# Reordered sums, copies and casts around seven-product units, and the last row statistic in three pieces, in a two-layer decoder trunk on one core

## The chip, the cores and the metric

The kernel runs on one core of one Trainium2 chip. Its time is the device time of one execution in microseconds; a comparison uses the median of several. The engines are named as in the profile: PE (TensorE), DVE (VectorE), ACT (ScalarE), POOL (GpSimd) and SP (SyncE, which issues most DMAs). Each engine works through its own queue in order, and waits where an operand is not ready.

## The reference, cut to what matters

```python
for i in range(2):
    h = h + 0.5 * swiglu(rmsnorm(h, norm_ffn1[i]), ffn1_w_in[i], ffn1_w_out[i])
    h = h + (retention if i == 0 else gla)(rmsnorm(h, norm_mix[i]), ...)
    h = h + 0.5 * swiglu(rmsnorm(h, norm_ffn2[i]), ffn2_w_in[i], ffn2_w_out[i])
return rmsnorm(h, final_norm)[:, 16:]

def swiglu(x, w_in, w_out):
    gate, up = split(x @ w_in, 2)
    return (silu(gate) * up) @ w_out
```

h has 528 rows (16 learned tokens and 512 of the input) of 1024 float32 values; the hidden width of swiglu is 2816, 22 tiles of 128. So there are four feed-forward blocks, called f10, f20, f11 and f21 in order of time, with retention after f10 and gated linear attention after f11.

## The kernel before, in words

Everything is kept transposed: features on the 128 partitions, tokens along the free dimension, in two halves of 264 (in f21 of 256). A float32 product is made of three products in a reduced format: a matrix is cast to a high part (ACT, L187: whi) and the rest is subtracted (DVE, L188: wlo); PE multiplies high by high (L487), high by low (L488) and low by high (L489).

Most products are taken in pairs of weight tiles by a scheme that needs seven block products instead of eight. Such a group is a *unit*. Its products have the names a11, s1, s2, a12, s4, s3, a22: sums of blocks of the weights (the tile `pair` holds two such sums, added up by a POOL DMA, L154; L194 and L196 make two more out of raw tiles) times sums of blocks of the activations. In a feed-forward block there are gate units ("g"), u units ("u", the up half) and o units ("o", the output). A product of a g or u unit is four tiles of three PE products, 12 in all.

The results of the seven lie in three pieces of PSUM: a bank X and two halves of QZ. X is used four times in a unit: a11, s2, s3 and a22 in turn. So X has to be read before the next of these can begin: a11 and s2 are copied to scratch by ACT (L734, L729), s1 by L727; s3 and a22 are read straight into a sum. The scratch tile is called su or szf. Three callbacks take the sums: `row1` after s4 (reads scratch and QZ), `c22` after s3 (reads X and scratch), `c21` after a22 (reads X). In a u unit `row1` adds (L1022) and multiplies by the gate's row (L1023), `c22` adds (L1030) and multiplies (L1031), `c21` is L1034. In an o unit `c22` adds scratch (L1068) and then X (L1069) to the residual x, and `c21` is L1073. The seventh product, a22, of a held unit stands on PE behind the next unit's a11 and s1. In the order of most units s4 comes before s3; in the last u unit of a block s3 comes first.

After each product `step` calls `hook()`, which fetches weights some products ahead (their casts and splits, L187 and L188), and then takes the results. Results are issued at high priority. In a block's very first unit the copies are issued ahead of the fetch, and the casts are told to stand behind the copy (`W.after`). A scheduler lays the instructions out in each engine's queue by these priorities and by when it takes their operands to be ready.

At the end (`out_last`) the rest of the last o products is taken in two halves of the tokens. For the second half each of the eight tiles x[d] is squared by ACT (L1190), and DVE adds the squares up (L1193) except the last; PE transposes the gained tiles (L1242) into yt, and column sums of the summed squares and of the last square, two PE instructions each, give the row statistic st_fb (L1249). After it come its root on POOL (L461), the scaling (ACT L1266 for rows 0 to 127, DVE L1268 for the others) and the writes (L1269).

Of the kernel before, what the change touches and what calls it, by code (L numbers as in the profile page):

```python
# [268 lines left out]
def trunk(ctx, tc, a):  # L269
# [422 lines left out]
    def unit_steps(key, name, order, halves, ks, rhs, places, row1, c22, c21, behind=None, done=None):  # L692
# [49 lines left out]
        def step(q, part=None):  # L742
# [72 lines left out]
    def ffn(which, layer, halves, gcol, u, feed, late=False):  # L815
# [7 lines left out]
        with tc.tile_pool(name=f"h_{me}", bufs=1) as hp, tc.tile_pool(name=f"t_{me}", bufs=1) as tp, \  # L823
# [187 lines left out]
            def unit_u(f, g, first):  # L1011
                y = []
# [6 lines left out]
                def row1(ab, qz):  # L1019
                    begin()  # L1020
                    o = y[0][:, 2:]
                    V.tensor_add(o, ab, qz)  # L1022
                    V.tensor_mul(o, o, pair(g[0], halves))  # L1023
# [3 lines left out]
                def c22(c, s):  # L1027
                    begin()
                    o = y[0][:, 1]
                    V.tensor_add(o, c, s)  # L1030
                    V.scalar_tensor_tensor(o, o, -1.0, g[1][:, b0:b1], ALU.mult, ALU.mult)  # L1031

# [14 lines left out]
            def unit_o(gi, d, behind):  # L1047
# [18 lines left out]
                def c22(c, s):  # L1066
                    o = x[d + 1][:, b0:b1]
                    V.scalar_tensor_tensor(o, s, 0.5, o, ALU.mult, ALU.add)  # L1068
                    V.scalar_tensor_tensor(o, c, 0.5, o, ALU.mult, ALU.add)  # L1069
# [102 lines left out]
    def out_last(key, hh, hl, halves, scale):  # L1172
# [10 lines left out]
        def evac(d, hf):  # L1183
# [4 lines left out]
            else:  # L1188
                t = tmp.tile([P, T], F32, tag="hf", name=f"sqf{hf}_{d}")
                S.activation(t[:, :wd], x[d][:, r0:r1], AF.Square)  # L1190
                if (d, hf) == (KD - 1, 1):
# [34 lines left out]
        later(1, lambda: later(1, rsqrt_rows(sqa[0][:, :wd], 1, D, "fa", first_half)[0]))  # L1226
        for d in range(KD - tail, KD):
# [5 lines left out]
            last = evac(d, 1)  # L1233
# [5 lines left out]

        def turn(d):  # L1240
            for j in range(2):
                nc.tensor.transpose(yt[j][:, d // 4, (d % 4) * P:(d % 4 + 1) * P], xg[d][:, j * P:(j + 1) * P], ident)  # L1242

        for d in range(KD - 4):
            turn(d)
        st = bank("st_fb")
        for i, sq in enumerate((sqa[1], last)):
            for j in range(2):
                ins = nc.tensor.matmul(st[:, j:j + 1], lhsT=sq[:, j * P:(j + 1) * P], rhs=ones[:, 0:1],  # L1249
                                       start=(i + j == 0), stop=(i == 1), skip_group_check=True)  # L1250
        with tc.issue_after(ins.ins):
            for d in range(KD - 4, KD):
# [5 lines left out]
        for b in range(2):  # L1258
            for j in range(2):
# [3 lines left out]
                for o in (0, 256) if b + j == 0 else (0,):  # L1263
                    c = slice(o, 256 + o if b + j == 0 else 512)
# [4 lines left out]
                    (nc.scalar if b + j == 2 else nc.sync).dma_start(  # L1269
# [1067 lines left out]
```

## Time and profile before

| | |
|---|---|
| three runs, us | 2020.34, 2024.03, 2027.34 (median 2024.03) |
| the profiled execution's own time, us | 2026.07 |
| its span, first to last instruction, us | 2024.3 |
| mean granted TensorE clock | 0.998 |
| DMA, mean over the span | 158 GB/s |

A row of the timeline has the start, the length, the engine, the line, the operation, what it writes and reads, and in brackets how long its engine idled before it and what ended that. A row of waits has the engine and tile that waited, what it waited for, the total in us, how many times, and the longest. PE is pipelined: a product is still shown when the next has started.

### The profile page before, as it was taken

How to read it: one execution, taken by the hardware profiler on the slowest of the kernel's cores; microseconds unless marked ns; L12 is line 12 of the kernel's file. 1: busy time of each engine (PE TensorE's matmuls, PEld its weight loads, DVE VectorE, ACT ScalarE, POOL GpSimd, SP SyncE). 2: the span in 40 equal slices, each digit the busy share in tenths (PEclk: the TensorE clock that was granted, in tenths of full speed). 3: DMA queues.
4: the chain of work that ended last, by engine and by line, in shares of the span. 5: the costliest groups of instructions: out<-in, count | busy, mean ns of one | idle time of the engine just before them, and what ended most of it. 6: DMA issues, size and time to landing. Idle time of an engine off the chain costs nothing.

```text
span 2024.3 us, 43498 instructions
## 1 busy us (share of the span) xinstructions
PE 1998.4 (99%) x16575; PEld 1965.3 (97%) x16575; DVE 1792.3 (89%) x3302; ACT 1192.3 (59%) x2427; POOL 209.9 (10%) x181
## 2 busy tenths in 40 slices
PE   9999999999999999999999999999999999999998
PEld 8999999999999999999999999999999989999998
DVE  8999999978787889989999998999997878988996
ACT  5666666554545465656666666667644544655664
POOL 1011111010101000111111011111001000111110
PEclk9999999999999999999999999999999999999999
DMA  7577777354645532776875477777624441687772
GB/s 227 136 198 178 200 192 185 109 146 132 159 129 147 136 115 74 191 191 161 214 188 162 128 190 187 179 199 178 187 65 119 112 135 63 165 202 183 181 189 68
DMA packets 176113, 318.87 MB, mean 158 GB/s; under 512 B 17568, under 2 KB 40736, under 8 KB 175904
## 3 DMA queue, kind: packets, MB, share of 16 engines
q1 hardware_dynamic: 133856, 237.04, 36.1%
q0 software_dynamic: 40896, 75.51, 23.4%
q10 hardware_dynamic: 1152, 3.55, 0.6%
q8 instruction: 130, 2.13, 0.4%
q14 instruction: 79, 0.65, 0.1%
HBM read 311.76 MB, written 4.26 MB: 156 GB/s over the span
## 4 chain that ended last, share of the span: by engine, by line
PE 80%; DVE 13%; ACT 2%; issue 2%; DMA 2%; POOL 0%; SPq 0%; POOLq 0%; DVEq 0%; ACTq 0%
DVE wlo L188 4%; PE po_r L488 1%; PE po_r L487 1%; PE po_r L489 1%; ACT whi L187 1%; PE lv L1857 1%; PE Xf11u L487 1%; PE Xf11u L489 1%; PE Xf11u L488 1%; PE Xf11g L487 1%; PE Xf11g L488 1%; PE Xf11g L489 1%; PE Xf20u L487 1%; DVE raw L196 1%; DVE hf L520 1%
## 5 line engine op out<-in xcount | busy, mean ns | idle before, releaser
L187 ACT CAST whi<-raw 128x512 fp32r<-128x512 f32 (+1 forms) x893 | 531.1, 606 | 415.0 <-DVE raw L196 151.4
L188 DVE TENSOR_TENSOR wlo<-raw,whi 128x512 fp32r<-128x512 f32 (+1 forms) x893 | 589.8, 668 | 101.2 <-ACT whi L187 88.6
L187 ACT CAST whi<-pair 128x512 fp32r<-128x512 f32 (+1 forms) x304 | 183.6, 604 | 77.4 <-issue 10.9
L188 DVE TENSOR_TENSOR wlo<-pair,whi 128x512 fp32r<-128x512 f32 (+1 forms) x304 | 201.7, 664 | 15.9 <-ACT whi L187 14.8
L154 POOL DMA_DIRECT2D pair<-in_f_in x73 | 89.0, 1220 | 714.7 <-DVE wlo L188 286.0
L194 DVE TENSOR_TENSOR raw<-pair,raw 128x512 f32<-128x512 f32 (+1 forms) x146 | 97.1, 665 | 5.7 <-DMA pair<-in_f_in 2.5
L196 DVE TENSOR_TENSOR raw<-raw,raw 128x512 f32<-128x512 f32 (+1 forms) x146 | 97.3, 666 | 3.2
L154 POOL DMA_DIRECT2D pair<-in_f_out x44 | 53.5, 1216 | 357.1 <-DVE wlo L188 101.0
L488 PE MATMUL po_r<-ogl,whi 128*128 128x264 f32 x256 | 71.3, 278 | 0.0
L487 PE MATMUL po_r<-ogh,whi 128*128 128x264 f32 x256 | 71.2, 278 | 0.0
L489 PE MATMUL po_r<-ogh,wlo 128*128 128x264 f32 x256 | 71.2, 278 | 0.0
L154 POOL DMA_DIRECT2D pair<-in_ret_in x20 | 24.4, 1222 | 300.6 <-DVE wlo L188 138.3
L997 ACT ACTIVATE gf<-gf 128x528 f32<-128x528 f32 (+1 forms) x36 | 23.2, 643 | 50.6 <-DVE gf L996 50.4
L487 PE MATMUL Xf10o<-hf,whi 128*128 128x264 f32 x176 | 49.6, 282 | 1.0 <-ACT szf L734 0.4
L487 PE MATMUL Xf20o<-hf,whi 128*128 128x264 f32 x176 | 49.4, 281 | 1.1 <-ACT szf L734 0.4
L487 PE MATMUL Xf11o<-hf,whi 128*128 128x264 f32 x176 | 49.4, 280 | 1.1 <-ACT szf L734 0.4
L488 PE MATMUL Xf10o<-hf,whi 128*128 128x264 f32 x176 | 49.1, 279 | 0.0
L488 PE MATMUL Xf20o<-hf,whi 128*128 128x264 f32 x176 | 49.1, 279 | 0.0
L488 PE MATMUL Xf11o<-hf,whi 128*128 128x264 f32 x176 | 49.1, 279 | 0.0
L489 PE MATMUL Xf10o<-hf,wlo 128*128 128x264 f32 x176 | 48.9, 279 | 0.0
L489 PE MATMUL Xf20o<-hf,wlo 128*128 128x264 f32 x176 | 48.9, 279 | 0.0
L489 PE MATMUL Xf11o<-hf,wlo 128*128 128x264 f32 x176 | 48.9, 279 | 0.0
(1182 smaller groups left out, 8602.6 us busy)
## 6 DMA issues: line engine op xcount, KB each, us to landing
raw<-in_f_in SPq DMA_DIRECT2D x277, 256.0 KB, 3.4
pair<-in_f_in SPq DMA_DIRECT2D x150, 256.0 KB, 5.1
pair<-in_f_in POOLq DMA_DIRECT2D x73, 512.0 KB, 7.7
raw<-in_f_out SPq DMA_DIRECT2D x80, 256.0 KB, 3.4
raw<-in_ret_in SPq DMA_DIRECT2D x76, 256.0 KB, 3.1
raw<-in_f_out SPq DMA_DIRECT2D x72, 192.0 KB, 3.0
pair<-in_f_out SPq DMA_DIRECT2D x48, 256.0 KB, 4.9
pair<-in_f_out POOLq DMA_DIRECT2D x24, 512.0 KB, 6.5
```

Source lines behind the costliest of these rows:

```text
L154: nc.gpsimd.dma_start(t, aps[2].unsqueeze(1).broadcast_to([P, 2, n]), accum_op=ALU.add)
L187: act = self.nc.scalar.copy(hi[:, :n], raw)
L188: dve = V.tensor_sub(lo[:, :n], raw, hi[:, :n].bitcast(F32))
L194: V.tensor_add(s2, self.tiles[c][:, 1], self.tiles[c, "a11"])
L196: V.tensor_add(raw, raw, s2)
L487: nc.tensor.matmul(ps, lhsT=lh, rhs=rh, start=start, stop=False, **kw)
L488: nc.tensor.matmul(ps, lhsT=lh, rhs=rl, start=False, stop=False, **kw)
L489: return nc.tensor.matmul(ps, lhsT=ll, rhs=rh, start=False, stop=stop, **kw)
L520: return S.copy(hi, src), V.tensor_sub(lo, src, hi.bitcast(F32))
L997: S.activation(o, o, AF.Silu, scale=-1.0)
L1857: nc.tensor.matmul(ps[:, j, J * P:J * P + n], lhsT=Kt[:, j, J * P:(J + 1) * P], rhs=q, start=(J == 0), stop=(J == 3), skip_group_check=True)
```

## The change: what it does

1. In g and u units of every block, the copies of s1, a11 and s2 are issued before the fetch, and the fetched casts are put behind the copy, as it was in a block's first unit alone.
2. In a u unit in which s4 comes first, `row1` takes only its addition; the multiplication by the gate's row is taken in `c22`, after that callback's own addition and multiplication.
3. In an o unit `c22` adds X first and scratch second.
4. At the end the square of tile 6 is kept apart, like that of tile 7 (in another scratch tile), so st_fb takes three pairs of column sums. The first stands between the transposes of tiles 0, 1 and 2, 3, the others behind those of 2, 3, and the transposes of tiles 4 to 7 stay behind all of them.
5. The first 512 columns of the last 128 rows are scaled and written in two halves, and the write that ACT's queue issues is now that of the last 512 columns of its own rows; before it was DVE's.

```diff
-            if first and q in ("s1", "a11", "s2"):
-                ends["copy"] = W.after = results(q)
+            if (first or key[2:3] == ("i",)) and q in ("s1", "a11", "s2"):
+                W.after = results(q)
+                if first:
+                    ends["copy"] = W.after
                 hook()
                 W.after = None
...
             def unit_u(f, g, first):
-                y = []
+                y, due = [], []
...
                     V.tensor_add(o, ab, qz)
+                    if not due:
+                        due.append(o)
+                        return
                     V.tensor_mul(o, o, pair(g[0], halves))
...
                     V.tensor_add(o, c, s)
                     V.scalar_tensor_tensor(o, o, -1.0, g[1][:, b0:b1], ALU.mult, ALU.mult)
+                    for o in due:
+                        V.tensor_mul(o, o, pair(g[0], halves))
+                    due.append(None)
...
                 def c22(c, s):
                     o = x[d + 1][:, b0:b1]
+                    V.scalar_tensor_tensor(o, c, 0.5, o, ALU.mult, ALU.add)
                     V.scalar_tensor_tensor(o, s, 0.5, o, ALU.mult, ALU.add)
-                    V.scalar_tensor_tensor(o, c, 0.5, o, ALU.mult, ALU.add)
...
-                t = tmp.tile([P, T], F32, tag="hf", name=f"sqf{hf}_{d}")
+                t = tmp.tile([P, T], F32, tag="sg" if (d, hf) == (KD - 2, 1) else "hf", name=f"sqf{hf}_{d}")
                 S.activation(t[:, :wd], x[d][:, r0:r1], AF.Square)
-                if (d, hf) == (KD - 1, 1):
+                if d >= KD - 2 and hf:
                     return t
...
-        for d in range(KD - 4):
-            turn(d)
         st = bank("st_fb")
-        for i, sq in enumerate((sqa[1], last)):
-            for j in range(2):
-                ins = nc.tensor.matmul(st[:, j:j + 1], lhsT=sq[:, j * P:(j + 1) * P], rhs=ones[:, 0:1],
-                                       start=(i + j == 0), stop=(i == 1), skip_group_check=True)
-        with tc.issue_after(ins.ins):
-            for d in range(KD - 4, KD):
+        ins = None
+        squares = [sqa[1]] + squares[-2:]
+        for n, (d0, d1) in enumerate(((0, 2), (2, 4), (4, KD))):
+            if n < 2:
+                for d in range(d0, d1):
+                    with behind([ins] if ins else []):
+                        turn(d)
+            with behind(turned[-1:]):
+                for j in range(2):
+                    ins = nc.tensor.matmul(st[:, j:j + 1], lhsT=squares[n][:, j * P:(j + 1) * P], rhs=ones[:, 0:1],
+                                           start=(n + j == 0), stop=(n == 2), skip_group_check=True)
+        with behind([ins]):
+            for d in range(4, KD):
                 turn(d)
...
-                for o in (0, 256) if b + j == 0 else (0,):
-                    c = slice(o, 256 + o if b + j == 0 else 512)
+                for o in (0, 256) if b == 0 else (0,):
+                    c = slice(o, 256 + o if b == 0 else 512)
...
-                    (nc.scalar if b + j == 2 else nc.sync).dma_start(
+                    (nc.scalar if b and not j else nc.sync).dma_start(
```

How the queues change, at the three places of which the prediction speaks. In the changed kernel L1024 is the addition that was L1022, L1038 the deferred multiplication that was L1023, L1035 and L1036 are what L1030 and L1031 were, and L1076 and L1077 what L1069 and L1068 were.

DVE, in block f20, at the second u unit after the plain tiles (its bank X is Xf20u_11610), before:

```order
L188 TENSOR_TENSOR wlo_11720<-raw_11352,whi_11719 128x512
L188 TENSOR_TENSOR wlo_11741<-raw_11426,whi_11740 128x512
L188 TENSOR_TENSOR wlo_11764<-raw_11471,whi_11763 128x512
L196 TENSOR_TENSOR raw_11471<-raw_11471,raw_11426 128x512
L1022 TENSOR_TENSOR su_11725<-su_11612,QZf20u_11611 128x2x264
L188 TENSOR_TENSOR wlo_11784<-raw_11471,whi_11783 128x512
L1023 TENSOR_TENSOR su_11725<-su_11725,gf_11449 128x2x264
L1030 TENSOR_TENSOR su_11725<-Xf20u_11610,su_11612 128x264
L188 TENSOR_TENSOR wlo_11803<-pair_11371,whi_11802 128x512
L1031 SCALAR_TENSOR_TENSOR su_11725<-su_11725,gf_11450 128x264
```

and now:

```order
L188 TENSOR_TENSOR wlo_11720<-raw_11353,whi_11719 128x512
L1024 TENSOR_TENSOR su_11725<-su_11612,QZf20u_11611 128x2x264
L188 TENSOR_TENSOR wlo_11740<-raw_11426,whi_11739 128x512
L1035 TENSOR_TENSOR su_11725<-Xf20u_11610,su_11612 128x264
L1038 TENSOR_TENSOR su_11725<-su_11725,gf_11449 128x2x264
L1036 SCALAR_TENSOR_TENSOR su_11725<-su_11725,gf_11450 128x264
L664 TENSOR_TENSOR t0f20h_11812<-su_11725 128x528
L188 TENSOR_TENSOR wlo_11765<-raw_11472,whi_11764 128x512
L665 SCALAR_TENSOR_TENSOR t1f20h_11813<-su_11725,t0f20h_11812 128x264
L196 TENSOR_TENSOR raw_11472<-raw_11472,raw_11426 128x512
```

Both sums moved up past two splits and L196, the multiplication moved behind the reading of X, and the sums of the hidden tile (L664, L665) moved up past splits as well.

ACT, in block f21, at the first u unit after the plain tiles (Xf21u_24552), before:

```order
L727 COPY su_24554<-QZf21u_24553 128x256
L187 CAST whi_24624<-raw_24419 128x512
L187 CAST whi_24642<-pair_24373 128x512
L187 CAST whi_24658<-raw_24357 128x512
L734 COPY su_24554<-Xf21u_24552 128x256
L187 CAST whi_24679<-raw_24419 128x512
```

and now:

```order
L727 COPY su_24554<-QZf21u_24553 128x256
L187 CAST whi_24588<-raw_24341 128x512
L187 CAST whi_24603<-pair_24258 128x512
L734 COPY su_24554<-Xf21u_24552 128x256
L187 CAST whi_24625<-raw_24419 128x512
L187 CAST whi_24642<-pair_24373 128x512
L187 CAST whi_24658<-raw_24357 128x512
```

The copy that empties X moved up past three casts, one of them of a pair tile.

DVE, in block f10, at the last o unit (Xf10o_4822), before:

```order
L1061 SCALAR_TENSOR_TENSOR x_81<-szf_4824,x_81 128x528
L591 TENSOR_TENSOR sqa_n_213<-sqa_n_213,sq_n_5_4991 128x528
L188 TENSOR_TENSOR wlo_4899<-raw_4574,whi_4898 128x512
L188 TENSOR_TENSOR wlo_4918<-raw_4648,whi_4917 128x512
L1069 SCALAR_TENSOR_TENSOR x_82<-Xf10o_4822,x_82 128x264
L188 TENSOR_TENSOR wlo_4940<-raw_4695,whi_4939 128x512
```

and now (L1069 is here what L1061 was):

```order
L1069 SCALAR_TENSOR_TENSOR x_81<-szf_4824,x_81 128x528
L591 TENSOR_TENSOR sqa_n_213<-sqa_n_213,sq_n_5_4991 128x528
L188 TENSOR_TENSOR wlo_4875<-raw_4555,whi_4874 128x512
L188 TENSOR_TENSOR wlo_4899<-raw_4574,whi_4898 128x512
L1076 SCALAR_TENSOR_TENSOR x_82<-Xf10o_4822,x_82 128x264
L188 TENSOR_TENSOR wlo_4918<-raw_4648,whi_4917 128x512
L1077 SCALAR_TENSOR_TENSOR x_82<-szf_4824,x_82 128x264
```

The split wlo_4918 moved behind the reading of X, wlo_4875 came in ahead of it, and the scratch's sum (L1077; L1068 stood several rows earlier) now follows.

More of the change, by code (lines that the diff above doesn't have):

```diff
@@ L1226, in out_last @@
         later(1, lambda: later(1, rsqrt_rows(sqa[0][:, :wd], 1, D, "fa", first_half)[0]))
+        squares = [sqa[1]]
         for d in range(KD - tail, KD):
@@ L1232, in out_last @@
             hook()
-            last = evac(d, 1)
+            squares.append(evac(d, 1))
             gained(d)
@@ L1238, in out_last @@
         yt = [acc_tile(f"yt{j}") for j in range(2)]
+        turned = []
         def turn(d):
             for j in range(2):
[L1242 to L1245 removed]
+                ins = nc.tensor.transpose(yt[j][:, d // 4, (d % 4) * P:(d % 4 + 1) * P], xg[d][:, j * P:(j + 1) * P], ident)
+            turned.append(ins)
         st = bank("st_fb")
[L1247 to L1252 removed]
+        ins = None
[11 more added lines that the diff above has]
+            for d in range(4, KD):
                 turn(d)
```

## The prediction

> **What bounds the kernel now.** The page comes first: one core, so its span is the time, and the busy shares say which engine to look at.
>
> ```profile
> span 2024.3 us, 43498 instructions
> ...
> PE 1998.4 (99%) x16575; PEld 1965.3 (97%) x16575; DVE 1792.3 (89%) x3302; ACT 1192.3 (59%) x2427; POOL 209.9 (10%) x181
> ```
>
> TensorE (PE) carries the kernel, and none of its products is removed. So only the places where PE stands still can be won. The timeline shows what "still" means. Products of 264 columns start 0.12 us apart (842.10, 842.22), although each row is 0.28 long:
>
> ```profile
> 840.82 1.89 DVE L188 TENSOR_TENSOR wlo<-raw,whi 128x512 fp32r<-128x512 f32 x3
> ...
> 842.10 0.28 PE L487 MATMUL Xf20g<-uhf,whi 128*128 128x264 f32 x1
> 842.22 0.28 PE L488 MATMUL Xf20g<-ulf,whi 128*128 128x264 f32 x1
> ...
> 842.75 0.69 DVE L196 TENSOR_TENSOR raw<-raw,raw 128x512 f32<-128x512 f32 x1
> 843.36 0.70 DVE L1022 TENSOR_TENSOR su<-su,QZf20u 128x528 f32<-128x528 f32 x1
> ...
> 844.20 0.69 DVE L188 TENSOR_TENSOR wlo<-raw,whi 128x512 fp32r<-128x512 f32 x1 [0.15 <-ACT whi L187]
> 844.81 0.70 DVE L1023 TENSOR_TENSOR su<-su,gf 128x528 f32<-128x528 f32 x1
> 845.43 0.42 DVE L1030 TENSOR_TENSOR su<-Xf20u,su 128x264 f32<-128x264 f32 x1
> ...
> 845.91 0.39 PE L487 MATMUL Xf20u<-thf,whi 128*128 128x264 f32 x1 [0.85 <-DVE su L1030]
> ```
>
> An idle bracket is counted from a product's end, 0.28 after its start; the next could have started 0.12 after it. So each break costs 0.16 us more than its bracket. The view of PE's waits lists the breaks by what ended them (total, times, longest):
>
> ```profile
> PE Xf21u L487 <- DVE su L1030: 1.2, 1, 1.2
> PE Xf11u L487 <- DVE su L1030: 1.2, 2, 0.9
> PE Xf20u L487 <- DVE su L1030: 1.1, 2, 0.8
> ...
> PE Xf21u L487 <- ACT su L734: 0.7, 1, 0.7
> PE QZf21u L487 <- ACT whi L187: 0.7, 1, 0.7
> ...
> PE Xf11o L487 <- ACT szf L734: 0.4, 1, 0.4
> PE Xf20o L487 <- ACT szf L734: 0.4, 1, 0.4
> PE Xf10o L487 <- ACT szf L734: 0.4, 1, 0.4
> ...
> PE Xf20o L487 <- DVE x L1069: 0.3, 1, 0.3
> PE Xf10o L487 <- DVE x L1069: 0.3, 1, 0.3
> PE Xf11o L487 <- ACT whi L1738: 0.3, 1, 0.3
> ...
> PE QZf10u L489 <- DVE wlo L188: 0.2, 1, 0.2
> ```
>
> The breaks are few and short, so the change can win single microseconds at best. 0.3% of the time, 6.1 us, is about the least that a measurement of this kernel tells from no change.
>
> **Part 1: the sum ahead of the gate's product, in u units.** In the timeline above PE wants bank X for the unit's seventh product, and VectorE must first take s3's result out of it (L1030). VectorE is in order: three splits, L196, L1022 and L1023 stand before L1030, and none of the splits is needed by that product. s3's products are over 0.16 after those of the next unit start, so at 842.3. In the new order the queue up to L1030's twin holds one split less before the first sum, no L196 and no multiplication. Counted from 840.82 with the rows' durations: one split to 841.5, the sum L1024 to 842.2, one split to 842.9, L1035 to 843.3. PE asks for the bank only after twelve products of Xf20g and twelve of QZf20g, 24 x 0.117 us after 842.10, at 844.9. So this break closes with some 1.6 us to spare.
>
> The same row of waits has five such breaks, 1.2 + 1.2 + 1.1 = 3.5 us in brackets, and 5 x 0.16 = 0.8 behind them: 4.3 us. The late thing after that is what was pushed back: the deferred product (0.70), the splits and L196, on which s4's weight of the next gate unit hangs. Between s3's end and s4 PE has five groups of twelve products, 5 x 1.4 = 7 us; the new queue puts about ten operations of 0.42 to 0.70 us in front of that split, some 6 us. So I count nothing for it here.
>
> **Part 2: copies ahead of casts, in g and u units.** The break of Xf21u behind L734 has this timeline:
>
> ```profile
> 1786.87 0.62 ACT L187 CAST whi<-pair 128x512 fp32r<-128x512 f32 x1 [2.81 <-issue]
> ...
> 1787.92 0.36 ACT L734 COPY su<-Xf21u 128x256 f32<-128x256 f32 x1
> ...
> 1788.33 0.39 PE L487 MATMUL Xf21u<-thf,whi 128*128 128x256 f32 x1 [0.75 <-ACT su L734]
> ```
>
> ScalarE stood 2.81 us before a cast, and the copy that frees X stood behind it. The row names no releaser; the cast's source is a tile that DMAs fill and add up, so I take that load to have been late. With the copy first, PE no longer waits for it: 0.7 + 0.16 = 0.9 us. The other side: a copy waits for its own products, and all casts queued behind it wait along, each 0.62, with VectorE's split (0.68) behind each. Where weights lie microseconds ahead that costs nothing. Where they don't, it shows as PE waiting for whi or wlo, as it does already in the first units of blocks f10 and f21 (the rows of 0.7 and 0.2). VectorE is the tight engine there, as the busy times of two stretches show (after the stretch: its length, then PE, weight load, VectorE, ScalarE, GpSimd):
>
> ```profile
> 60.00:95.00 35.00, 33.80 (x283) 33.08 (x282) 33.96 (x59) 24.05 (x50) 3.66 (x3) 1.00 0.63 157
> ...
> 825.00:860.00 35.00, 34.10 (x288) 33.90 (x289) 33.74 (x60) 23.95 (x49) 4.00 (x4) 1.00 0.76 184
> ```
>
> VectorE is 97% and 96% busy, so time cannot be made there, only moved. No row shows the new queue's price. From below it is nothing; from above it is one late cast with its split, 1.3 us, in each of the two tight first groups' three unit pairs, 7.8 us. I take 0.8, nearer to the bottom, because the breaks there now are 0.2 and 0.7.
>
> So of parts 1 and 2, 4.3 + 0.9 = 5.2 us lie open; I take 4.5, since a break that closes often leaves a few tenths.
>
> **Part 3: bank before scratch, in o units.** The last o units of f10, f20 and f11 have two breaks each. One in f10:
>
> ```profile
> 343.36 1.29 DVE L188 TENSOR_TENSOR wlo<-raw,whi 128x512 fp32r<-128x512 f32 x2
> 344.56 0.42 DVE L1069 SCALAR_TENSOR_TENSOR x<-Xf10o,x 128x264 f32<-128x264 f32 x1
> ...
> 345.13 0.36 PE L487 MATMUL Xf10o<-hf,whi 128*128 128x264 f32 x1 [0.31 <-DVE x L1069]
> ```
>
> L1069 reads the bank and stood behind two splits; in the new order its twin has the second of them, and the scratch's sum, behind it. The break of f11 is put down to another cast (L1738) but lies at the same place. In the L734 rows the copy stood behind casts and activations, and the new ScalarE order has one cast less before it. The six rows sum to 3 x 0.4 + 3 x 0.3 = 2.1, with 6 x 0.16 = 1.0 behind them: 3.1 us. Bounds: 3.1 won, or nothing, if the splits pushed back become the next wait. I take half, 1.5.
>
> **Part 4: the end.** PE's last work runs so:
>
> ```profile
> 2015.34 1.04 PE L1242 MATMUL yt<-ident,endh 128*128 128x128 f32 x8
> ...
> 2015.88 0.42 DVE L1193 TENSOR_TENSOR endh<-endh,sqf 128x256 f32<-128x256 f32 x1
> 2016.06 0.42 ACT L1190 ACTIVATE sqf<-x 128x256 f32<-128x256 f32 x1
> 2016.35 0.61 PE L1249 MATMUL st_fb<-ones,endh 128*128 128x1 f32 x4
> ...
> 2016.82 0.58 PE L1249 MATMUL st_fb<-ones,sqf 128*128 128x1 f32 x4
> 2017.26 1.07 PE L1242 MATMUL yt<-ident,endh 128*128 128x128 f32 x8
> ...
> 2019.88 0.40 SPq L1269 DMA_DIRECT2D out<-yb  x1
> ...
> 2020.38 0.45 SPq L1269 DMA_DIRECT2D out<-endl  x1
> ```
>
> Eight transposes take until 2016.21 (1.04 less the 0.17 by which a product outlasts its slot). Then PE waits 0.14 for the sum L1193 (over at 2016.30) and takes two pairs of column sums, 0.47 and 0.44. The change removes the last L1193 and adds a third pair. PE is then never idle, but has 0.87 + 3 x 0.45 = 2.22 us of work where 1.92 passed before: 0.3 us later, since the last square (2016.48) is not what PE waits for. And SP's queue gets one more write ahead of its last: its writes are 0.50 apart. Bounds: +0.3 if the last bytes land as before, +0.8 if the whole step shows. I take +0.4, because the same bytes are moved.
>
> [...]
>
> **The sum.** -4.5 + 0.8 - 1.5 + 0.4 = -4.8 us. The profiled execution took 2026.07 (1.8 outside its span), so it would take 2021.3. That execution lay 2.0 above the median of the three runs, 2024.03, so the median would be 2019.2: 0.24% less.
>
> **The rivals.**
> *All of it closes.* For it: the u break has 1.6 us to spare, and PE's bank is what each of these rows names. Against it: VectorE is 96% busy where the f20 ones lie. It gives 5.2 + 3.1 less the end's 0.4, and about 1 us more where breaks too short for this list close: -9, 2015. Chance 0.2.
> *VectorE pays it back.* The time is only moved: in the tight stretches the split of a weight becomes the next wait, and what PE gains at the bank it loses some products later. For it: 33.96 of 35 us. Against it: in f20 only 0.15 us of VectorE's idling before a split is seen. It gives about 0 (-1.5 to +2), 2024. Chance 0.18.
> *The copies block the casts (slower).* ScalarE's casts queue behind copies that wait for PE, three per unit. It decides once a weight is ready less than one cast and split, 1.3 us, before its use. Six such breaks more than cancel the sum; with the 7.8 of part 2 taken whole in place of 0.8 it is +2.2, and with the 5.2 and 1.5 not won either, at +8: 2032. Against it: ScalarE is 59% busy. Chance 0.08.
>
> **How the numbers follow.** My sum has 0.54. Its own range is -8 to -2, and a quarter of it lies beyond -6.1. Faster by over 0.3%: 0.2 and 0.14 of mine, 0.34. Slower by over 0.3%: 0.08. Within: 0.58. The range leaves out the deep end of the first rival and the slower one: 2013.5 to 2025.5.
>
> **What would show it.** Right: the waits of Xf20u, Xf11u and Xf21u for the sum on X gone, and that of Xf21u for L734's copy; in the timeline the sum starts within 0.5 us of the end of s3's products; three pairs of column sums at the end, without a gap. Wrong: new rows of PE waiting for whi or wlo in the first groups (VectorE pays back, or the casts are blocked); the o rows still there; or the third pair at 0.1 us.

## The result and the profile after

The changed kernel took 2039.12 us (median of 6 runs, 2035.83 to 2041.63). The kernel before took 2024.03 beside it, the median of five runs (2020.34 to 2027.40); a sixth took 9586.55 and is left out (with it the median is 2025.68). The ratio is 1.0074, with a 95% interval of 1.0059 to 1.0089: 0.74% slower, about 15 us. The forecast was 2019.2, and the range ended at 2025.5.

First the head of the changed kernel's page: the span, and the busy time of each engine with its share and its instructions.

```profile
span 2039.9 us, 43481 instructions
...
PE 2008.3 (98%) x16579; PEld 1972.2 (97%) x16579; DVE 1791.4 (88%) x3302; ACT 1180.8 (58%) x2427; POOL 210.0 (10%) x181
```

VectorE's work is the same (1791.4 after 1792.3), PE has four instructions more, and the span is 15.6 us longer. PE's idle time grew from 25.9 to 31.6 us, and its busy time by 9.9: a product is shown for longer than its slot (0.28 us, where the next starts 0.12 behind it), so a delay below 0.16 us counts as busy time, and so does a product at half the clock (last section). PE's waits in the changed kernel (total, times, longest) say where it stands still:

```profile
PE pg_gz L1762 <- ACT whi L1755: 3.0, 1, 3.0
...
PE QZf11o L487 <- ACT su L727: 1.7, 1, 1.7
PE QZf20o L487 <- ACT su L727: 1.5, 1, 1.5
...
PE QZf21o L487 <- ACT su L727: 1.1, 2, 0.7
...
PE pq L487 <- ACT uhret L573: 0.9, 1, 0.9
...
PE QZf20u L489 <- DVE wlo L188: 0.5, 1, 0.5
```

The five breaks of the u units on the sum over X, and the one behind L734's copy in f21, are gone from the list. New are waits in the *middle* of o units of f20 and f11 (QZ for L727's copy; f21 had one of 0.9 before), and waits at the entry of the stage behind a block (pg_gz behind f11, pq behind f10). The row of QZf20u is new too; there are like ones of 0.4 for f10 (0.2 before) and f11. They lie in the blocks' first groups.

Put product beside product in the two traces (the k-th product of one form in one with the k-th in the other), the growth of PE's lateness stands at few places, given by before's time. Lost: 1.7 us at 20 to 40, 4.6 at 320 to 360 (end of f10, entry of retention), 1.1 at 400 to 420 (in retention), 2.0 at 960 to 980, 3.0 at 1060 to 1120 (end of f20), 2.0 at 1300 to 1320, 3.3 at 1380 to 1440 (end of f11), 1.0 at 1940 to 1960. Won: 1.2 at 840 to 860, 1.15 at 1180 to 1200, 2.4 at 1780 to 1800, which are the u units of f20, f11 and f21. In the first group of f10 (60 to 300), where the forecast had put its price, the lateness moves by at most 0.5.

A u unit of f20 in the changed kernel, VectorE's queue:

```profile
849.89 0.68 DVE L188 TENSOR_TENSOR wlo<-raw,whi 128x512 fp32r<-128x512 f32 x1
850.49 0.70 DVE L1024 TENSOR_TENSOR su<-su,QZf20u 128x528 f32<-128x528 f32 x1
851.11 0.69 DVE L188 TENSOR_TENSOR wlo<-raw,whi 128x512 fp32r<-128x512 f32 x1
851.71 0.42 DVE L1035 TENSOR_TENSOR su<-Xf20u,su 128x264 f32<-128x264 f32 x1
852.05 0.70 DVE L1038 TENSOR_TENSOR su<-su,gf 128x528 f32<-128x528 f32 x1
```

L1035 empties X at 852.13, one split ahead of it, and PE takes up the bank at 853.4 without a wait: that break closed as worked out, though the sum starts 1.0 us after the end of s3's products (850.7) and not within the 0.5 us that was named as a sign. What the same change took away is the lead of the weights. Here is ScalarE around the copies L729, L727 and L734 of one u unit of f20, first before:

```profile
1022.58 0.36 ACT L729 COPY su<-Xf20u 128x264 f32<-128x264 f32 x1
1022.84 0.62 ACT L187 CAST whi<-pair 128x512 fp32r<-128x512 f32 x1
1023.37 0.62 ACT L187 CAST whi<-raw 128x512 fp32r<-128x512 f32 x1
1023.88 0.62 ACT L187 CAST whi<-pair 128x512 fp32r<-128x512 f32 x1
1024.40 0.38 ACT L727 COPY su<-QZf20u 128x264 f32<-128x264 f32 x1
...
1026.63 0.37 ACT L734 COPY su<-Xf20u 128x264 f32<-128x264 f32 x1
```

and the same unit in the changed kernel:

```profile
1031.56 0.36 ACT L729 COPY su<-Xf20u 128x264 f32<-128x264 f32 x1
1031.81 0.62 ACT L187 CAST whi<-raw 128x512 fp32r<-128x512 f32 x1
1032.44 0.38 ACT L727 COPY su<-QZf20u 128x264 f32<-128x264 f32 x1
1033.92 0.62 ACT L187 CAST whi<-raw 128x512 fp32r<-128x512 f32 x1 [1.10 <-DVE raw L196]
...
1035.25 0.37 ACT L734 COPY su<-Xf20u 128x264 f32<-128x264 f32 x1
1035.52 0.62 ACT L187 CAST whi<-raw 128x512 fp32r<-128x512 f32 x1
```

The names carry no numbers here; the order of the program's instructions gives them. Before, the casts of weights 599, 600 and 601 stand between L729 and L727, and those up to 603 ahead of L734. Now only 597 stands between the first two, and 599 is the last ahead of L734: four weights fewer. Weight 600, split on VectorE and first read by PE (L489), before and in the changed kernel:

```profile
1024.11 0.68 DVE L188 TENSOR_TENSOR wlo<-raw,whi 128x512 fp32r<-128x512 f32 x1
...
1029.96 0.28 PE L489 MATMUL Xf20g<-uhf,wlo 128*128 128x264 f32 x1
```

```profile
1036.17 0.69 DVE L188 TENSOR_TENSOR wlo<-raw,whi 128x512 fp32r<-128x512 f32 x1 [0.30 <-ACT whi L187]
...
1039.47 0.28 PE L489 MATMUL Xf20g<-uhf,wlo 128*128 128x264 f32 x1
```

The split was over 5.2 us ahead of its use (1029.96 less 1024.79), now 2.6. I call this time the weight's *lead*. Worked out in the same way for all the 63 to 84 weights of a kind of unit, matched by number, the medians in block f20 are (the tenth percentile for o units in brackets):

| kernel | g | u | o |
|---|---|---|---|
| before | 5.97 | 4.88 | 5.13 (2.28) |
| changed | 2.06 | 2.09 | 3.13 (0.65) |

The medians of the other blocks lie within 0.4 us of these. A tied cast waits for its copy, and the copy for PE; its split and the buffers of its raw tile wait along. So loads are issued later too: in stretches of 40 us of the four blocks the median load of a raw tile is up to some 4.5 us later against PE than before, and the median POOL DMA that fills a pair tile mostly 1 to 5 us.

### The profile page after: what moved, and what is told of

Same layout as the page of the kernel before. It is cut to its first block, busy times and chain, and to the rows that moved or that the text cites. A ratio compares the mean times of both kernels' runs of the same rounds, so it can differ in the third digit from the quotient of the medians.

```text
span 2039.9 us, 43481 instructions
## 1 busy us (share of the span) xinstructions
PE 2008.3 (98%) x16579; PEld 1972.2 (97%) x16579; DVE 1791.4 (88%) x3302; ACT 1180.8 (58%) x2427; POOL 210.0 (10%) x181
## 3 DMA queue, kind: packets, MB, share of 16 engines
q8 instruction: 130, 2.13, 0.4%
## 4 chain that ended last, share of the span: by engine, by line
PE 77%; DVE 14%; DMA 4%; ACT 2%; issue 2%; POOL 0%; SPq 0%; DVEq 0%; ACTq 0%; POOLq 0%
DVE wlo L188 4%; PE po_r L487 1%; PE po_r L488 1%; PE po_r L489 1%; DVE hf L520 1%; ACT whi L187 1%; PE lv L1874 1%; DMA raw<-in_f_in 1%; DMA pair<-in_f_in 1%; PE Xf21o L487 1%; PE Xf21o L488 1%; PE Xf21o L489 1%; PE Xrg L487 1%; PE Xf21u L487 1%; PE Xrg L489 1%
## 5 line engine op out<-in xcount | busy, mean ns | idle before, releaser
L194 DVE TENSOR_TENSOR raw<-pair,raw 128x512 f32<-128x512 f32 (+1 forms) x146 | 97.0, 665 | 7.8 <-issue 5.8
L196 DVE TENSOR_TENSOR raw<-raw,raw 128x512 f32<-128x512 f32 (+1 forms) x146 | 97.3, 666 | 2.6
L489 PE MATMUL po_r<-ogh,wlo 128*128 128x264 f32 x256 | 71.2, 278 | 0.0
L489 PE MATMUL Xf20o<-hf,wlo 128*128 128x264 f32 x176 | 48.8, 281 | 0.6 <-DVE wlo L188 0.6
L489 PE MATMUL Xf10o<-hf,wlo 128*128 128x264 f32 x176 | 48.8, 280 | 0.3 <-DVE wlo L188 0.2
L489 PE MATMUL Xf11o<-hf,wlo 128*128 128x264 f32 x176 | 48.8, 280 | 0.2 <-DVE wlo L188 0.2
L488 PEld LDWEIGHTS po_r<-ogl,whi 128*128 128x128 f32 x256 | 48.1, 188 | 0.0
```

What stands on the lines that cost most here:

```text
L194: V.tensor_add(s2, self.tiles[c][:, 1], self.tiles[c, "a11"])
L196: V.tensor_add(raw, raw, s2)
L488: nc.tensor.matmul(ps, lhsT=lh, rhs=rl, start=False, stop=False, **kw)
L489: return nc.tensor.matmul(ps, lhsT=ll, rhs=rh, start=False, stop=stop, **kw)
```

## The experiments

The first question was which part does it. Theory A put it on the swap in the o units, since the new waits lie there and at the ends of o rows. Its rivals put it on the copies ahead of casts (B) or on the deferred products (C). Four kernels take one part each.

**Part 1 alone.**

```diff
-            if first and q in ("s1", "a11", "s2"):
-                ends["copy"] = W.after = results(q)
+            if (first or key[2:3] == ("i",)) and q in ("s1", "a11", "s2"):
+                W.after = results(q)
+                if first:
+                    ends["copy"] = W.after
                 hook()
                 W.after = None
```

> The kernel before with part 1 alone: in g and u units the copies of s1, a11 and s2 are issued ahead of the fetch, and the casts behind the copy. The changed kernel lost about 15 us, and its trace shows the loads of weights issued 2.5 to 5 us later against PE through the four feed-forward blocks. Theory A (the swapped sums of the o units push the splits of weights back, and so the loads): this part alone gives between -2 and +2 us. Theory B (the copies hold the casts back, each cast its split, each split the buffer that the next load waits for): this part alone gives +8 to +15 us, with the loads late in the o units too. By the forecast's sum: about 0 (0.9 won, 0.8 paid).

Measured: 2041.12 us, ratio 1.0081 (1.0064 to 1.0098), +16.4 us. Median leads in f20: g 2.11, u 2.06, o 2.99 (tenth percentile 0.25). PE's waits have the changed kernel's rows again:

```profile
PE pg_gz L1747 <- ACT whi L1740: 2.2, 1, 2.2
...
PE QZf11o L487 <- ACT su L727: 1.4, 1, 1.4
```

Theory B holds and A falls: this part alone makes as much as the whole loss, a little more than B's +15. The o units have no tie, and lose their lead all the same.

**Part 2 alone.**

```diff
                     V.tensor_add(o, ab, qz)
+                    if not due:
+                        due.append(o)
+                        return
                     V.tensor_mul(o, o, pair(g[0], halves))
...
                     V.scalar_tensor_tensor(o, o, -1.0, g[1][:, b0:b1], ALU.mult, ALU.mult)
+                    for o in due:
+                        V.tensor_mul(o, o, pair(g[0], halves))
+                    due.append(None)
```

> The kernel before with part 2 alone: the multiplication by the gate's row in the u units is taken after the sum that reads X. Both theories A (o units' swap is what costs) and B (copies ahead of casts is what costs): -3 to -5 us, since the four breaks of the u units on the sum over X close as they did in the changed kernel (1.2 us there at two places and 2.4 at a third). A third theory, C: the deferred multiplication with the sums of the hidden tile stands ahead of the splits in VectorE's queue, so that it is this part that makes the loads late: +2 to +10 us, with the breaks closed all the same.

Measured: 2023.25 us, ratio 0.9991 (0.9981 to 1.0002), -1.5 us beside the run's before by the medians, -1.8 by the ratio. Leads in f20 4.90, 5.80 and 4.96 (u, g, o). The breaks are down to 0.2 each for f11 and f20, and f21's row is gone. C falls. The breaks close, but the gain is smaller than expected and not clear of no change.

**Part 3 alone.**

```diff
                     o = x[d + 1][:, b0:b1]
+                    V.scalar_tensor_tensor(o, c, 0.5, o, ALU.mult, ALU.add)
                     V.scalar_tensor_tensor(o, s, 0.5, o, ALU.mult, ALU.add)
-                    V.scalar_tensor_tensor(o, c, 0.5, o, ALU.mult, ALU.add)
```

> The kernel before with part 3 alone: in the o units X is added before the scratch. Theory A: +8 to +14 us, with the loads in the o rows issued 3 us or more later against PE than before, and the new waits at the entry of the stages behind f10, f20 and f11. Theories B and C: between -2 and +1 us. By the forecast's sum: -1.5 us.

Measured: 2028.86 us, ratio 1.0022 (1.0013 to 1.0031), +4.4 us. That lies between the theories: too little for A, and the wrong sign for the forecast. The leads don't move (4.87, 5.97, 5.06). Nor did the breaks that the swap was to close: all six rows still stand at 0.3 to 0.4, with L1068 now the line that reads X:

```profile
PE Xf20o L487 <- DVE x L1068: 0.3, 1, 0.3
```

In its trace one place grew by much, the entry behind f11, on ScalarE and PE:

```profile
1428.74 0.62 ACT L187 CAST whi<-raw 128x512 fp32r<-128x512 f32 x1 [1.32 <-DMA raw<-in_gla_in]
1429.26 0.73 ACT L573 ACTIVATE uhgla<-x,gains 128x528 fp32r<-128x528 f32 x1
...
1432.86 2.27 PE L620 MATMUL st_n<-ones,sqa_n 128*128 128x1 f32 x10 [2.20 <-DVE sqa_n L591]
```

Before, that last row was:

```profile
1431.54 1.25 PE L620 MATMUL st_n<-ones,sqa_n 128*128 128x1 f32 x10 [0.82 <-DVE sqa_n L591]
```

A cast waits for a load, the normalized rows stand behind the cast, and the wait of the column sums is 1.4 us longer. PE also ran at half its clock behind this entry: 0.66 of the full clock is the mean of 1432 to 1442, where before has 1.00 (last section).

**Parts 4 and 5 alone.**

```diff
-                if (d, hf) == (KD - 1, 1):
+                if d >= KD - 2 and hf:
                     return t
...
-        for i, sq in enumerate((sqa[1], last)):
+        for n, (d0, d1) in enumerate(((0, 2), (2, 4), (4, KD))):
```

(with the rest of the end as in the change above.)

> The kernel before with parts 4 and 5 alone: the last two squares kept apart, three pairs of column sums, the first 512 columns of the last rows written in two halves. All theories: +0.3 to +0.8 us, which a comparison of this kernel can hardly tell from none; in the profile the last product ends 0.3 us later after the last square than before. By the forecast's sum: +0.4 us.

Measured: 2024.93 us, ratio 0.9998 (0.9984 to 1.0012): no difference. In this kernel no instruction of the u units has moved, and yet a wait of the u units in f21 is not what it was before (1.2):

```profile
PE Xf21u L487 <- DVE su L1030: 0.3, 1, 0.3
```

and the row of Xf21u behind L734 (0.7 before) isn't there. So these two breaks of before differ from one execution to the next; the next kernel's trace has 1.2 and 0.3 for them.

**The tie or the order.** Part 1 does two things: it issues the copy ahead of the fetch, and it ties the fetched casts behind the copy. One kernel takes the order alone:

```diff
-                W.after = results(q)
+                ins = results(q)
                 if first:
-                    ends["copy"] = W.after
+                    ends["copy"] = W.after = ins
                 hook()
```

(against part 1 alone.)

> The kernel before with half of part 1: the copies of s1, a11 and s2 issued ahead of the fetch in every g and u unit, but the casts of the fetch not told to stand behind the copy (W.after stays as before, for a block's first unit alone). Part 1 whole gave +16 us, and cut the lead of a weight's split over its first use from 4.9 to 6.0 us (median of a kind of unit) to 2 to 3. Theory B1 (the tie holds each cast back until PE has finished the product and the copy has run): without the tie +-2 us from before, leads above 4. Theory B2 (the place in the issue order is enough, since the scheduler gives the queue to what was issued first): again +10 to +16 us, leads of 2 to 3.

Measured: 2024.28 us, ratio 1.0005 (0.9996 to 1.0014); leads 5.97, 4.87 and 5.13. ScalarE's instructions at the unit shown above stand as before, row by row. So the tie makes the loss and the order nothing; the copies are taken at high priority anyway.

**The tie in u units alone.**

```diff
-            if (first or key[2:3] == ("i",)) and q in ("s1", "a11", "s2"):
+            if (first or key[2:4] == ("i", "u")) and q in ("s1", "a11", "s2"):
```

> The kernel before with part 1 in u units alone, g units as before. If each tied copy costs its share of the lead, and a weight's lead is refilled over the units that are not tied, then about half of the 16 us, +5 to +10, with a short lead in u units and a longer one in g units. If one tied kind of unit is enough to keep all later weights late (the lead isn't made up again because VectorE is 96% busy): +12 to +16, with leads of 2 to 3 us in g and o units too.

Measured: 2037.1 us, ratio 1.007 (1.0056 to 1.0083), +14.2 us; leads of g 2.70, u 2.13, o 3.25. Half the ties cost nearly the whole: a lead once lost isn't made up in the units between.

**The changed kernel without part 1** (the condition `first` alone, as before; all else as changed).

```diff
-            if (first or key[2:3] == ("i",)) and q in ("s1", "a11", "s2"):
-                W.after = results(q)
-                if first:
-                    ends["copy"] = W.after
+            if first and q in ("s1", "a11", "s2"):
+                ends["copy"] = W.after = results(q)
```

> The changed kernel without part 1: deferred multiplication, the o units' swap and the end. If part 1 is what made it slower, and the parts about add (measured alone: -1.8 for the deferral, +4.4 for the swap, 0 for the end): about +2.5 over before, between 0 and +5 us, with leads of 4.9 us and more as in before. If the changed kernel's loss needs the other parts as well (the deferral pushes splits back under any order): +8 us or more.

Measured: 2027.31 us, ratio 1.0024 (1.0011 to 1.0036), +4.9 us; leads as before. So of the changed kernel's 15 us the tie makes about 10. The rest is near what the swap gave alone (4.4), but then the 1.8 of the deferral is missing from it: the parts don't simply add.

**The lead by look-ahead.** If the lead is what counts, more look-ahead must give it back.

```diff
-AHEAD = 4
+AHEAD = 5
```

> The changed kernel with the fetch one product further ahead (AHEAD 5 in place of 4), everything else as changed. Theory: the loss is the lost lead of the weights, by which casts, splits and loads come a product later, so one product more of look-ahead, some 1.4 us, gives back much of the loss: 5 to 12 us less than the changed kernel, leads of 3.5 us and more. Rival: the leads are set by the two engines' time and by how many tiles of weights there are, not by the look-ahead: within 3 us of the changed kernel, leads unchanged.

Measured: 2029.47 us, ratio 1.0037 (1.0024 to 1.0051); leads g 3.84, u 3.90, o 4.39. Half the loss is gone. With 6:

> The changed kernel with AHEAD 6. With 5 it came from +15 to +7.5 us. If each product of look-ahead gives back one product's lead (leads went from 2.1 to 3.9 us with the first): leads of 4.9 us and more, and -1 to +4 us from before. If the number of weight tiles (7) limits the look-ahead: leads as with 5, +6 to +9 us.

Measured: 2026.61 us, ratio 1.0019 (1.0011 to 1.0028); leads 5.00, 4.68 and 4.98, near those of before, and 3.8 us from its time. Leads and times move together in these three kernels. The control is the kernel before with AHEAD 5:

> The kernel before with the fetch one product further ahead (AHEAD 5 in place of 4) and nothing else: the control for the run in which that gave back half of the changed kernel's loss. If the look-ahead helps only by replacing the lead that part 1 took away, the kernel before has lead enough: within 3 us of before, either way. If a longer look-ahead is a gain of its own: 4 us or more faster. If it costs (buffers and queues in another order): 4 us or more slower, so that the 7 us given back in the changed kernel were more than the lead's share.

Measured: 2018.71 us, ratio 0.9973 (0.9962 to 0.9984), 5.5 us faster. The longer look-ahead is a gain of its own. It leaves the medians of the leads (6.22, 4.95, 5.23) but lifts the shortest: the tenth percentile in u units of f20 goes from 2.55 to 4.08. In its list of PE's waits no row of a u unit and none of L727 is left. So the 7.5 us that it won in the changed kernel need not all be lead given back.

**Where the swap costs.** Two kernels take it in block f11 alone, and in the three others:

```diff
-                    V.scalar_tensor_tensor(o, s, 0.5, o, ALU.mult, ALU.add)
-                    V.scalar_tensor_tensor(o, c, 0.5, o, ALU.mult, ALU.add)
+                    for t in (c, s) if me == "f11" else (s, c):
+                        V.scalar_tensor_tensor(o, t, 0.5, o, ALU.mult, ALU.add)
```

> The kernel before with the o units' swap in block f11 alone. The swap in all blocks gave +4.4 us (0.22%). In its trace the one place that grew by much is the entry of the linear attention behind f11 (1420 to 1490 us): a load of the next stage's weights is issued later, a cast waits 1.32 us for it, the normalized rows stand behind that cast, the column sums of the squares wait 2.2 us in place of 0.8, and two or three windows of 3.41 us at half the clock follow. Theory S1 (this place is the whole price of the swap): +3 to +6 us, with the wait of the column sums at 2 us or more. Theory S2 (the swap costs a little at every o unit): +0.5 to +1.5 us, a quarter of 4.4.

Measured: 2024.42 us, ratio 1.0005 (0.9996 to 1.0014). And with `me != "f11"`:

> The kernel before with the o units' swap in blocks f10, f20 and f21, not in f11. Theory S1 (the entry behind f11 is the whole price): within 1.5 us of before, or up to 1.5 us faster, as the forecast had it for part 3. Theory S2 (a little at every o unit): +3 to +4 us.

Measured: 2026.8 us, ratio 1.0011 (1.0003 to 1.002). Theory S1 falls: f11 alone gives +1.0, the others +2.2. Together they make 3.2 of 4.4, within the intervals, so S2, a little everywhere, is the better of the two. What pays it isn't settled. The trace of the second is of its shortest execution (2021.23, against a median of 2026.8), so it doesn't show what the longer ones pay. And the two traces with the swap in all blocks and without the tie each have three pieces of half clock behind f11, some 5 us, where before has none and the swap in f11 alone one: the swap's price may be these.

**Late loads alone.**

```diff
-    def __init__(self, tc, ctx, raw_bufs=7, pair_bufs=3, bufs=7):
+    def __init__(self, tc, ctx, raw_bufs=6, pair_bufs=3, bufs=7):
```

> The kernel before with 6 buffers for raw weight tiles in place of 7: no tie, no other order of the sums, but each load has to wait for its buffer one tile longer. If late loads alone make the changed kernel's breaks (a cast waits for a DMA, a copy stands behind it, PE waits for the copy): +8 to +20 us, with the new waits of the changed kernel at QZ of the o units (su, L727) and at the entries of the stages. If not the loads but the casts' place behind the copies is what costs: within 3 us of before.

Measured: 2034.19 us, ratio 1.0048 (1.0032 to 1.0063). It is slower, but not as either theory had it. In the four blocks the raw tiles' loads are 2.5 to 4 us later against PE for the most part, as in the changed kernel, and yet the leads stayed (5.97, 4.87, 5.10) and the o units have no new wait; the pair tiles' POOL DMAs hardly moved there (medians mostly within 1.3 us). The time went at the entries and in retention, 5.3 us of it at the entry behind f11, where ScalarE shows:

```profile
1434.16 0.62 ACT L187 CAST whi<-raw 128x512 fp32r<-128x512 f32 x1 [2.36 <-DMA raw<-in_gla_in]
```

So late raw tiles alone cost at the entries, where loads are waited for, and not in the o units. By exclusion, what hurts those is late pair tiles together with a short lead; no run makes the pair tiles late alone.

**The copies of the o units ahead too.**

```diff
-            if (first or key[2:3] == ("i",)) and q in ("s1", "a11", "s2"):
+            if (first or key[2:3] in (("i",), ("o",))) and q in ("s1", "a11", "s2"):
```

> The changed kernel with part 1 in the o units as well: their copies of s1, a11 and s2 ahead of the fetch, and the casts tied to them. If the mid-o breaks are copies that stand behind a cast whose load is late, they go: PE's waits for L727 in the o units (1.7, 1.5 and 1.1 us) vanish, worth 2 to 5 us, unless the further loss of lead in the o units costs as much at the entries. If lead is the one thing that counts: 4 to 12 us slower than the changed kernel, with leads of 2 us or less in the o units.

Measured: 2031.61 us, ratio 1.0049 (1.0035 to 1.0063), some 5 us less than the changed kernel's 1.0074, though the leads in o units fall to 1.66. PE's waits now:

```profile
PE pg_gz L1762 <- ACT whi L1755: 2.8, 1, 2.8
...
PE pq L487 <- ACT uhret L573: 1.4, 1, 1.4
...
PE Xf20o L489 <- DVE wlo L188: 0.9, 2, 0.5
```

All L727 rows are gone, and the waits for the split itself grow, to 0.9 us each in f10, f20 and f11 from 0.2, 0.6 and 0.2. So in the middle of the o units it was the place of the copy behind a late cast; the waits at the entries stay.

**The parts that pay.** The changed kernel without the swap and with the copies ahead but not tied, then the same with AHEAD 5 (the edits are those above).

> The changed kernel without the tie of the casts to the copies and without the o units' swap: the deferred multiplication, the copies issued ahead of the fetch but not tied, and the end are left. By the sum of the parts measured alone (-1.8, +1.0, about 0): -2 to 0 us from before. By the forecast's terms for what is left (3.5 won of the u units' breaks, +0.4 at the end): -3.

Measured: 2021.03 us, ratio 0.9987 (0.9979 to 0.9996).

> The parts that pay (deferred multiplication, copies issued ahead without the tie, the end; no swap in the o units) with AHEAD 5. The two were measured apart at -2.6 and -5.5 us. If they add: -7 to -9 us. If the longer look-ahead closes the same breaks of the u units as the deferral does: -5 to -6 us.

Measured: 2018.76 us, ratio 0.9979 (0.9969 to 0.9988). The gains don't add: the look-ahead closes the u units' breaks by itself. The kernel before with AHEAD 5, 0.9973, beats both kernels, and the deferral on top of it (0.9979) can't be told from it.

## Why the prediction was wrong

**Parts 1 and 2, what they win.** The mechanism was right: the u breaks closed. The size was too large. The deferral alone measured -1.8 us (by the ratio, with no change just inside its interval) where 3.5 + 0.8 = 4.3 lay open. Some 1.4 of that, the f21 row, and the 0.9 for the row of L734 could not be counted on: in the kernel with the end alone the first was 0.3 and the second missing, and ScalarE idled 0.54 us before the cast of the pair tile where it had idled 2.81. So both seem to hang on when a DMA landed in one execution. I had read this from the row itself ("I take that load to have been late") and still counted it as lasting.

**Part 1, what it costs: the step that failed.** "Where weights lie microseconds ahead that costs nothing", and then a price of 0.8 us for the tight first groups, at most 7.8. The measured price is 16.4 us. The new waits for wlo in the first groups, named as a sign of being wrong, did come in the changed kernel, but they are 0.4 to 0.5 us each, and in f20 and f11 PE's lateness falls there all the same. Nearly all of the price lies elsewhere. Leads of 5 to 6 us looked like cover that a wait of one cast would leave alone. But the tie binds three casts in seven to PE's progress, and fell together with what VectorE makes of them (L194 and L196 write tiles that later casts read: the 1.10 us idle above): the lead shrank to 2 us and stayed there, also in the o units that were not tied. There it met pair tiles that fill late. In the middle of an o row of f20, the cast of one weight (566) before, and the same place in the changed kernel:

```profile
975.85 0.62 ACT L187 CAST whi<-pair 128x512 fp32r<-128x512 f32 x1 [0.16 <-ACT su L729]
```

```profile
985.39 0.28 PE L489 MATMUL Xf20o<-hf,wlo 128*128 128x264 f32 x1
986.16 0.69 DVE L194 TENSOR_TENSOR raw<-pair,raw 128x512 f32<-128x512 f32 x1 [2.07 <-issue]
986.24 0.62 ACT L187 CAST whi<-pair 128x512 fp32r<-128x512 f32 x1 [2.86 <-DMA raw<-in_f_in]
...
986.76 0.37 ACT L727 COPY su<-QZf20o 128x264 f32<-128x264 f32 x1
...
987.19 0.39 PE L487 MATMUL QZf20o<-hf,whi 128*128 128x264 f32 x1 [1.52 <-ACT su L727]
```

ScalarE idles 2.86 us before the cast, in place of 0.16. The L194 on VectorE, which reads the same pair tile, starts within 0.1 us of it. So I take the tile to have filled only then, whatever the row names as releaser. The copy that PE waits for had its operands but stands behind the cast, and PE idled 1.52 us until it was over. This is the break of Xf21u behind L734 over again, which the change was to remove, in a kind of unit that its condition leaves out.

At the entry of retention it is the casts for the next stage, before and in the changed kernel:

```profile
345.18 1.30 ACT L187 CAST whi<-raw 128x512 fp32r<-128x512 f32 x2 [0.37 <-DMA raw<-in_ret_in]
```

```profile
350.76 1.26 ACT L187 CAST whi<-raw 128x512 fp32r<-128x512 f32 x2 [2.78 <-DMA raw<-in_ret_in]
351.93 1.36 ACT L573 ACTIVATE uhret<-x,gains 128x528 fp32r<-128x528 f32 x2
...
352.71 0.39 PE L487 MATMUL pq<-uhret,whi 128*128 128x264 f32 x1 [0.94 <-ACT uhret L573]
```

The same casts idle 2.78 us in place of 0.37, and the normalized rows that PE needs stand behind them.

**The rival "the copies block the casts"** named the right mechanism, with a chance of 0.08. Its place (the first groups), its price (up to 7.8 us for the tie) and its point of decision ("less than one cast and split") were taken from how long one cast takes, not from what the whole queue loses. Against it I had held that ScalarE is 59% busy. A share of busy time says nothing about a queue that is told to wait: ScalarE was 58% busy after. The order rows that I quoted for f21 showed it: the copy had moved past three casts, and I read that as the copy's gain only.

**Part 3**: the forecast had -1.5 and bounds of -3.1 to nothing. Alone it measured +4.4 us. Two things failed. The breaks didn't close: they stand in every trace with the swap and without the tie, and they are gone from the trace of part 1 alone, which has no swap. And the upper bound was nothing, while the swap has a price.

**Part 4**: the step holds in kind. In the changed kernel the end on PE is:

```profile
2030.69 0.60 PE L1253 MATMUL yt<-ident,endh 128*128 128x128 f32 x4
2031.12 0.50 PE L1266 MATMUL st_fb<-ones,endh 128*128 128x1 f32 x4
2031.49 0.63 PE L1253 MATMUL yt<-ident,endh 128*128 128x128 f32 x4
2031.96 0.95 PE L1266 MATMUL st_fb<-ones,sqf 128*128 128x1 f32 x8
2032.77 1.07 PE L1253 MATMUL yt<-ident,endh 128*128 128x128 f32 x8
```

There is no gap, and 2.08 us from the first of these to the last transposes, where 1.92 passed before: 0.16 later, half of the 0.3 worked out, since a pass takes 0.10 us here (0.81 by eight). No run shows the 0.1 us that stood for the third pair as a sign of being wrong: four passes took 0.44 before (the second pair), and take 0.37 here (2031.12 to 2031.49). On the whole time it shows nothing (0.9998).

**The sum.** The parts measured alone give 16.4 - 1.8 + 4.4 - 0.4 = 18.6 us, the whole about 15: they overlap by some 4 us.

**Two readings to set right.** The timeline of the u break has four splits before L1030, not three; the way out of it is the same. And the second stretch shown as tight, 825 to 860, lies in f20, while the text named f10 and f21. It changes nothing: in the first 25 us of f21, 1735 to 1760, VectorE is busy for 24.13.

## What to carry to other kernels

Casts tied behind copies that wait for the bottleneck engine lost their lead here (medians of 5.97 and 4.88 us in g and u units fell to 2.06 and 2.09), and the lead was missing in the next kind of unit too (5.13 to 3.13 in o units, which were not tied). So measure how far ahead of its use each prefetched tile is finished, at the median and at the tenth percentile, before and after. A break that stands in one trace may be absent in the next execution (Xf21u behind L1030: 1.2 us before, 0.3 with the end alone): count it as won only if two executions show it. Before reordering around such breaks, try one step more of look-ahead; here it closed those of the u units, at a ratio of 0.9973.

## What was not expected of the hardware

PE's clock falls to half in pieces of 3.41 us, and how many a run gets varies: by the clock events of the traces none ahead of the end in the kernel with the swap outside f11, one in before (at 21.3 us), two of them joined (6.83 us) at 20.1 and one at 354.6 in the changed kernel. Each costs about 1.7 us by estimate (half of 3.41, at half the rate), so 3.4 of the 15.6 us between the two spans are of this kind, the first 1.7 at the entry of f10, at which the change does nothing. After the entry behind f11 it shows in this stretch, before and with the swap alone (the length, PE, weight load, VectorE, ScalarE, GpSimd, then the clock, the DMA engines' busy share and GB/s):

```profile
1432.00:1442.00 10.00, 10.00 (x80) 9.52 (x81) 7.08 (x17) 4.22 (x8) 1.92 (x2) 1.00 0.85 271
```

```profile
1432.00:1442.00 10.00, 9.14 (x47) 8.69 (x47) 5.48 (x13) 2.25 (x4) 1.92 (x2) 0.66 0.83 215
```

47 products pass in place of 80. With the swap in f11 alone the same stretch kept its clock. In the changed kernel without part 1, which has the swap in all blocks, it lost it again (at 1433.0, and once more at 1480.8, as with the swap alone at 1432.7 and 1480.5). With the end alone it lost half as much (one piece, at 1432.7). So the execution decides in part, and whether the swap helps it along stays open.

A second variation is small and lasts: in f21 the same products of 256 columns start 0.1178 us apart in some stretches and 0.1167 in others. Before, 0.1167 turns into 0.1178 at a break (1867); in the changed kernel 0.1178 turns into 0.1167 at 1855 without one. One stretch before, and with the swap outside f11:

```profile
1900.00:1960.00 60.00, 60.00 (x512) 60.00 (x511) 55.60 (x107) 37.95 (x82) 8.44 (x7) 1.00 0.72 180
```

```profile
1900.00:1960.00 60.00, 60.00 (x516) 60.00 (x516) 55.55 (x106) 38.21 (x85) 8.13 (x7) 1.00 0.74 184
```

512 and 516 products in 60 us without a pause at the full clock: 1% of the rate, some 2 us over f21. What sets it stays open.
